# One-hot operands of an expert gate matrix: the first key's made by GpSimd instead of VectorE

## The chip, the cores and the metric

The kernel runs on one core of a Trainium2 chip, as one launch. The metric is the device time of one execution in microseconds, the median of several runs. TensorE, VectorE, ScalarE, GpSimd and SyncE each have an instruction queue of their own and run in its order; they meet at semaphores. In the profile they are PE (PEld is its weight load), DVE, ACT, POOL and SP.

## The reference, cut to what matters

A decoder layer for 1024 tokens (and 16 meta tokens) of width 1024 in float32: latent attention and retention side by side, merged, and then a mixer of 16384 single-neuron experts. The change lies in the mixer. Each token has 8 heads, and each head picks 16 experts by two keys, e1 and e2, from 0 to 127 each:

```python
q = (x @ w_peer_q).reshape(T, PEER_HEADS, PEER_DQ)
s1 = einsum('thd,kd->thk', q[..., :half], keys_1)      # 128 first keys
s2 = einsum('thd,kd->thk', q[..., half:], keys_2)      # 128 second keys
...
eidx = (e1 * 128 + e2).reshape(T, 8 * 16)              # 128 experts of one token
gates = softmax(sc).reshape(T, 8 * 16)
act = gelu(einsum('td,tkd->tk', x, peer_u[eidx]))
y = einsum('tk,tkd->td', gates * act, peer_v[eidx])
```

## The kernel before, in words

The 1024 tokens are 8 blocks of 128, in three groups: blocks 0 to 2, 3 and 4, 5 to 7. Attention, retention and merge run group after group. The experts are done in two ways.

*Blocks 0 to 2 gather.* For every token block and each of the 128 chosen experts, GpSimd issues an indirect DMA that fetches one row of peer_u or peer_v for each of the 128 tokens (`fetch` in `gathered`, L1065, tile `row`, 128 x 1024, four buffers, three fetched ahead). VectorE multiplies a row of peer_u with the tokens (L1082) or accumulates a row of peer_v into `acc` (L1087, `scalar_tensor_tensor` with `row` and `acc` as its two tiles). These VectorE instructions are pinned behind whatever was written to VectorE's queue just ahead of them (`keep_in_program_order`).

*Blocks 3 to 7 (640 tokens) are dense* (`dense`, L1128). For each first-key slice of 128 experts the scores of all 640 tokens are made by TensorE: the weights are split in a high part (`whi`, ScalarE, L218) and a low part (`wlo`, VectorE, L219), and three products (`mm3`, L246 to L248, tiles `tr`) are summed, in a 256-wide and a 384-wide piece; ScalarE applies the gelu (L1159). The scores of the first 48 slices are made ahead and stored to HBM (`gl_d`). Beside them the gate matrix is built: for each token a 128 x 128 matrix, first key by second key, with the gate where the token chose that expert. In the second half of `dense` the scores are multiplied with it (`gt`, read back from `gate_d`), and TensorE forms the output with peer_v (tiles `zacc`).

*The gate matrix* (`gate_matrix`, L1094) is a sum over the token's 128 choices, so it is a product: `oa` has for each choice (partition) a one at its first key, `ob` has the gate at its second key. Both compare a constant row of 0 to 127 (`iota`) with the key, a scalar for each partition (`kt`); `ob` multiplies with the gate (`gT`) as well. Of one token `oa` is the weight operand and `ob` the moving operand of TensorE's product (L1105, two instructions a token). Eight tokens make a step: two tiles `oa` and two `ob` of four tokens each, with four buffers each, so two steps fit. The products of a step are written after the operands of the next; ScalarE copies the result to `stage` (L1106), and every 32 tokens go to `gate_d` in one DMA from SyncE's queue.

*Order.* `pace` is called with a cost after each piece of foreground work and steps two background generators by credit: the routing and gate matrix of the dense blocks, and the gathers. A gate step yields 2.0, a gathered row 1.2. At the end of the 48 slices `finish(0)` drains what is left of the gate matrix. Within the dependencies the framework's scheduler then orders each engine's queue itself, by its own estimate of when an operand is ready; on TensorE the products of a token stand between score products.

Of the kernel before, what the change touches and what calls it, by code (L numbers as in the profile page):

```python
# [18 lines left out]
OP = mybir.AluOpType  # L19
# [124 lines left out]
def hybrid_layer(ctx: ExitStack, tc: tile.TileContext, out, a, dbg=None):  # L144
    nc = tc.nc
    V, S, T, G = nc.vector, nc.scalar, nc.tensor, nc.gpsimd
# [39 lines left out]
    def load_const(name, ap, shape):  # L186
        t = const.tile(shape, F32, name=name)
        nc.sync.dma_start(t, ap)
        return t
# [89 lines left out]
    def zacc(name="zacc"):  # L279
        return ps.tile([P, 2, 512], F32, name=name, tag="zacc", bufs=3)  # L280
# [813 lines left out]
    def gate_matrix(i, kt, gT, p):  # L1094

        stage = {}

        def products(t8, pairs):
            t0 = t8 // TS * TS
            if t8 == t0:  # L1100
                stage[0] = p.tile([P, P, TS], F32, name="stage", bufs=2)
            pg = zacc()
            for q, (oa, ob) in enumerate(pairs):
                for t in range(4):
                    T.matmul(pg[:, q, P * t:P * t + P], oa[:, t], ob[:, t], start=True, stop=True)  # L1105
            S.activation(stage[0][:, :, t8 - t0:t8 - t0 + 8].rearrange("p e (q t) -> p e q t", q=2),  # L1106
                         pg.rearrange("p q (t e) -> p e q t", t=4), AF.Copy)
            if t8 == t0 + TS - 8:
                nc.sync.dma_start(gate_d[(P * i + t0) // TS], stage[0].rearrange("p e t -> p (e t)"))

        pending = None
        for t8 in range(0, P, 8):
            pairs = []
            for q in range(2):
                oa = p.tile([P, 4, P], F32, name="oa", bufs=4)
                ob = p.tile([P, 4, P], F32, name="ob", bufs=4)
                for t in range(4):
                    k = t8 + 4 * q + t
                    V.tensor_scalar(oa[:, t], iota, kt[:, 0, k:k + 1], None, op0=OP.is_equal)  # L1119
                    V.tensor_scalar(ob[:, t], iota, kt[:, 1, k:k + 1], gT[:, k:k + 1], op0=OP.is_equal, op1=OP.mult)  # L1120
                pairs.append((oa, ob))
            if pending:
                products(*pending)
            pending = (t8, pairs)
            yield 2.0
        products(*pending)

    def dense(xT):  # L1128
# [33 lines left out]
        def routes():  # L1162

            kts, ktp = open_pool("ktl", "right")
            fcs, fc = open_pool("fcd", "right")
            n = len(last)
            top = top_tiles(n, fc)
            for h in range(H):
                first_top16(h, top, key_scores(queries(h, xT, n, fc), n))
                yield 1.85 * n  # L1170
            for i, b in enumerate(last):
                found = yield from choose(b, *top[i], fc, ktp)
                routed.append(found)
            fcs.close()
            pacing["rates"] = RATES[4]
            gms, gm = open_pool("gm")
            for i, (kt, gT) in enumerate(routed):
                yield from gate_matrix(i, kt, gT, gm)
            gms.close()
            kts.close()  # L1180
# [85 lines left out]
    iota = load_const("iota", a["c_iota"], [P, P])  # L1266
# [49 lines left out]
```

## Time and profile before

| | |
|---|---|
| median of 3 runs | 3613.85 us (3611.62 to 3617.17) |
| profiled execution | 3618.72 us, of which span 3616.9 us |
| busy: TensorE, VectorE, ScalarE, GpSimd | 3343.7, 2788.3, 1191.6, 1088.5 us |
| oa and ob (L1119, L1120) | 640 instructions each, from 1633.7 to 2037.1 us |

The span runs from the first instruction to the last. Busy time is the union of an engine's instructions, so instructions that overlap at their ends count once; a mean duration can then be longer than the distance from one start to the next. A TensorE instruction's end is modelled. The idle time of a group is that just before its instructions, with who released it.

### The profile page before, as it was taken

The numbers are of one execution on the slowest core, as the hardware profiler recorded it, in microseconds if no ns is written. First come the engines' busy times: TensorE is split into PE (matmuls) and PEld (weight loads), VectorE is DVE, ScalarE is ACT, GpSimd is POOL, SyncE is SP. The second block draws the span as 40 slices with busy tenths as digits, with TensorE's granted clock in tenths as the row PEclk, the third lists the DMA queues.
The fourth block names the chain that finished last, engine by engine and source line by source line (L and its number), as shares of the span: only waits on it lengthen the run. The fifth ranks groups of instructions, "written<-read, shape, count | busy, mean of one in ns | idle before, by whom it ended". The sixth has DMA issues, their size and how long they took to land.

```text
span 3616.9 us, 54537 instructions
## 1 busy us (share of the span) xinstructions
PE 3343.7 (92%) x20376; PEld 3023.5 (84%) x20376; DVE 2788.3 (77%) x6698; ACT 1191.6 (33%) x2017; POOL 1088.5 (30%) x772
## 2 busy tenths in 40 slices
PE   8999989998799998999898899999999989999999
PEld 7888988788677898998888687888788878887788
DVE  5645569997896666899999887787778777877776
ACT  3445334544355533233333222222222222222221
POOL 0000000112011121113333355454545544544454
PEclk9999999999899998999999999999999999999999
DMA  3322454467644376455666788898889888988886
GB/s 128 119 81 98 136 189 136 150 211 242 209 145 154 123 261 242 160 174 218 267 252 259 273 313 315 286 321 293 303 281 315 279 288 297 323 298 287 287 298 247
DMA packets 329257, 837.18 MB, mean 231 GB/s; under 512 B 45712, under 2 KB 140688, under 8 KB 326176
## 3 DMA queue, kind: packets, MB, share of 16 engines
q1 hardware_dynamic: 218400, 431.00, 35.4%
q0 software_dynamic: 110592, 402.70, 31.5%
q8 instruction: 160, 2.62, 0.3%
q14 instruction: 105, 0.86, 0.1%
HBM read 755.16 MB, written 78.43 MB: 230 GB/s over the span
## 4 chain that ended last, share of the span: by engine, by line
PE 42%; DVE 20%; issue 16%; DMA 11%; POOL 8%; ACT 3%; POOLq 0%; SPq 0%; DVEq 0%; ACTq 0%
PE zacc L246 9%; PE zacc L248 9%; PE zacc L247 9%; POOL row L1065 8%; DMA row<-in_peer_v_dram,eidx 7%; DVE ob L1120 4%; DVE oa L1119 3%; DVE wlo L219 3%; DVE acc L1087 3%; PE tr L246 3%; PE tr L247 2%; PE tr L248 2%; PE tr L765 2%; DMA gt<-gate_d 2%; PE sc L729 1%
## 5 line engine op out<-in xcount | busy, mean ns | idle before, releaser
L1065 POOL DMA_INDIRECT row<-in_peer_u_dram,eidx x384 | 494.6, 1288 | 1726.3 <-DVE row L1082 837.0
L218 ACT ACTIVATE whi<-raw 128x1024 fp32r<-128x1024 f32 (+2 forms) x508 | 520.7, 1026 | 1263.4 <-PE zacc L248 626.9
L219 DVE TENSOR_TENSOR wlo<-raw,whi 128x1024 fp32r<-128x1024 f32 (+2 forms) x508 | 599.3, 1180 | 328.4 <-ACT whi L218 327.3
L1065 POOL DMA_INDIRECT row<-in_peer_v_dram,eidx x384 | 593.7, 1546 | 772.9 <-DVE acc L1087 643.9
L246 PE MATMUL zacc<-whi,c_hi 128*128 128x512 f32 x1280 | 511.2, 399 | 75.3 <-ACT c_hi L218 59.2
L1087 DVE SCALAR_TENSOR_TENSOR acc<-row,dots,acc 128x1024 f32<-128x1024 f32 x384 | 481.7, 1279 | 92.9 <-DMA row<-in_peer_v_dram,eidx 92.2
L248 PE MATMUL zacc<-whi,c_lo 128*128 128x512 f32 x1280 | 509.1, 398 | 2.0 <-DVE c_lo L219 2.0
L247 PE MATMUL zacc<-wlo,c_hi 128*128 128x512 f32 x1280 | 507.9, 397 | 0.0
L1082 DVE SCALAR_TENSOR_TENSOR row<-row,xn 128x1024 f32<-128x1024 f32 x384 | 463.7, 1219 | 55.3 <-DMA row<-in_peer_u_dram,eidx 54.5
L246 PE MATMUL tr<-xT_hi,whi 128*128 128x384 f32 (+1 forms) x1216 | 417.0, 343 | 17.9 <-ACT gl L1159 16.8
L248 PE MATMUL tr<-xT_hi,wlo 128*128 128x384 f32 (+1 forms) x1216 | 413.9, 340 | 0.0
L247 PE MATMUL tr<-xT_lo,whi 128*128 128x384 f32 (+1 forms) x1216 | 411.8, 339 | 0.0
L246 PEld LDWEIGHTS zacc<-whi,c_hi 128*128 128x128 f32 x1280 | 246.9, 193 | 132.9 <-ACT c_hi L218 62.5
L248 PE MATMUL tr<-x_hi,wlo 128*128 128x256 f32 x1024 | 300.4, 293 | 37.3 <-DVE wlo L219 37.3
L246 PE MATMUL tr<-x_hi,whi 128*128 128x256 f32 x1024 | 299.5, 292 | 11.1 <-ACT whi L218 9.1
L247 PE MATMUL tr<-x_lo,whi 128*128 128x256 f32 x1024 | 297.0, 290 | 0.0
L248 PEld LDWEIGHTS zacc<-whi,c_lo 128*128 128x128 f32 x1280 | 245.7, 192 | 60.0 <-DVE c_lo L219 8.3
L247 PEld LDWEIGHTS zacc<-wlo,c_hi 128*128 128x128 f32 x1280 | 246.7, 193 | 51.3
L246 PE MATMUL zacc<-whi,hn_hi 128*128 128x256 f32 x832 | 251.5, 302 | 3.8 <-DVE vr L679 1.3
L246 PEld LDWEIGHTS tr<-xT_hi,whi 128*128 128x128 f32 x1216 | 232.4, 191 | 20.4 <-ACT gl L1159 18.0
L247 PE MATMUL zacc<-wlo,hn_hi 128*128 128x256 f32 x832 | 239.7, 288 | 1.4 <-DVE wlo L219 1.4
L248 PE MATMUL zacc<-whi,hn_lo 128*128 128x256 f32 x832 | 238.6, 287 | 0.0
(284 smaller groups left out, 6935.6 us busy)
## 6 DMA issues: line engine op xcount, KB each, us to landing
raw<-in_peer_ut_dram SPq DMA_DIRECT2D x128, 512.0 KB, 4.8
raw<-in_peer_vt_dram SPq DMA_DIRECT2D x128, 512.0 KB, 6.6
gate_d<-stage SPq DMA_DIRECT2D x20, 2048.0 KB, 7.4
gt<-gate_d SPq DMA_DIRECT2D x32, 1280.0 KB, 14.6
raw<-in_w_nat_dram SPq DMA_DIRECT2D x72, 512.0 KB, 3.5
raw<-in_w_z_dram SPq DMA_DIRECT2D x48, 512.0 KB, 3.3
gl_d<-gl SPq DMA_DIRECT2D x48, 320.0 KB, 2.2
gl<-gl_d SPq DMA_DIRECT2D x48, 320.0 KB, 6.3
```

The lines of the kernel that those rows point to most:

```text
L218: S.activation(hi, src, AF.Copy)
L219: V.tensor_tensor(lo, src, hi.bitcast(F32), OP.subtract)
L246: T.matmul(o, st[0], mv[0], start=first, stop=False)
L247: T.matmul(o, st[0], mv[1], start=False, stop=False)
L248: T.matmul(o, st[1], mv[0], start=False, stop=last)
L729: T.matmul(sc[:, c, 0:w], qh, kT[0:96, k0:k0 + w], start=True, stop=c < nch - 1)
L765: T.matmul(oo, vh[:, c + k], pT[:, k], start=False, stop=c + k == b)
L1065: G.indirect_dma_start(out=row, out_offset=None, in_=table, in_offset=bass.IndirectOffsetOnAxis(ap=eidx[:, k:k + 1], axis=0))
L1082: op = V.scalar_tensor_tensor(row, row, 1.0, xn, op0=OP.mult, op1=OP.mult, accum_out=dots[:, k:k + 1])
L1087: op = V.scalar_tensor_tensor(acc[k % 2], row, dots[:, k:k + 1], acc[k % 2], op0=OP.mult, op1=OP.add)
L1119: V.tensor_scalar(oa[:, t], iota, kt[:, 0, k:k + 1], None, op0=OP.is_equal)
L1120: V.tensor_scalar(ob[:, t], iota, kt[:, 1, k:k + 1], gT[:, k:k + 1], op0=OP.is_equal, op1=OP.mult)
```

## The change

One line. The `oa` tiles are filled by GpSimd instead of VectorE, with the same instruction, shape and operands; `ob` stays on VectorE, and nothing else is touched.

```diff
                 for t in range(4):
                     k = t8 + 4 * q + t
-                    V.tensor_scalar(oa[:, t], iota, kt[:, 0, k:k + 1], None, op0=OP.is_equal)
+                    G.tensor_scalar(oa[:, t], iota, kt[:, 0, k:k + 1], None, op0=OP.is_equal)
                     V.tensor_scalar(ob[:, t], iota, kt[:, 1, k:k + 1], gT[:, k:k + 1], op0=OP.is_equal, op1=OP.mult)
```

## Rows read from the trace of the kernel before

**Rows 1.** The page: busy time by engine, and GpSimd's row of the 40 slices.
```profile
PE 3343.7 (92%) x20376; PEld 3023.5 (84%) x20376; DVE 2788.3 (77%) x6698; ACT 1191.6 (33%) x2017; POOL 1088.5 (30%) x772
...
POOL 0000000112011121113333355454545544544454
```

**Rows 2.** Windows by stage: stretch, its length, busy time of each engine, clock, DMA.
```profile
core 0: us, PE busy (x) PEld busy (x) DVE busy (x) ACT busy (x) POOL busy (x), PEclk, DMA share, GB/s
1420.00:1633.00 213.00, 198.29 (x1250) 194.18 (x1249) 177.06 (x730) 67.86 (x101) 27.30 (x20) 0.96 0.50 169
1633.00:2040.00 407.00, 369.00 (x2606) 349.09 (x2605) 404.83 (x1378) 131.88 (x165) 130.72 (x70) 0.98 0.65 245
...
2170.00:3617.00 1447.00, 1360.11 (x7053) 1201.33 (x7051) 1106.66 (x1352) 334.68 (x454) 720.41 (x512) 0.97 0.85 295
```

**Rows 3.** Groups by line, 1633 to 2040 us: busy, mean ns | idle before, releasers.
```profile
L1120 DVE TENSOR_SCALAR ob<-iota,kt,gT 128x128 f32<-128x128 f32 x640 | 216.7, 339 | 0.0
L1105 PEld LDWEIGHTS zacc<-ob,oa 128*128 128x128 f32 x1280 | 186.9, 192 | 15.6 <-DVE ob L1120 8.3 <-issue 3.7 <-PE zacc L1105 0.4
L1119 DVE TENSOR_SCALAR oa<-iota,kt 128x128 f32<-128x128 f32 x640 | 182.2, 285 | 0.0
L1065 POOL DMA_INDIRECT row<-in_peer_v_dram,eidx x70 | 130.7, 1867 | 257.6 <-DVE acc L1087 245.4 <-DVE ob L1120 11.9 <-issue 0.3
L1087 DVE SCALAR_TENSOR_TENSOR acc<-row,dots,acc 128x1024 f32<-128x1024 f32 x72 | 88.5, 1274 | 2.2 <-DMA row<-in_peer_v_dram,eidx 2.2
...
L248 PE MATMUL tr<-x_hi,wlo 128*128 128x256 f32 x220 | 73.1, 332 | 35.5 <-DVE wlo L219 35.5
...
L219 DVE TENSOR_TENSOR wlo<-raw,whi 128x1024 fp32r<-128x1024 f32 x26 | 31.5, 1213 | 0.0
```

**Rows 4.** Chain of waits, 1633 to 2040 us, shares by line.
```profile
by line: DVE ob L1120 33.3%; DVE oa L1119 26.6%; DVE acc L1087 16.1%; issue 13.5%; DVE wlo L219 6.7%; DMA row<-in_peer_v_dram,eidx 3.4%; POOL row L1065 0.5%; DVEq L1087 0.0%; POOLq L1065 0.0%; DVEq L219 0.0%
```

**Rows 5.** Timeline of VectorE: start, length, then the instruction and its count.
```profile
1664.76 0.34 DVE L1120 TENSOR_SCALAR ob<-iota,kt,gT 128x128 f32<-128x128 f32 x1
1665.02 3.67 DVE L1087 SCALAR_TENSOR_TENSOR acc<-row,dots,acc 128x1024 f32<-128x1024 f32 x3
1668.61 1.22 DVE L219 TENSOR_TENSOR wlo<-raw,whi 128x1024 fp32r<-128x1024 f32 x1
1669.74 0.28 DVE L1119 TENSOR_SCALAR oa<-iota,kt 128x128 f32<-128x128 f32 x1
1669.94 0.34 DVE L1120 TENSOR_SCALAR ob<-iota,kt,gT 128x128 f32<-128x128 f32 x1
1670.19 0.28 DVE L1119 TENSOR_SCALAR oa<-iota,kt 128x128 f32<-128x128 f32 x1
```

**Rows 6.** Timeline of GpSimd in the same microseconds.
```profile
1666.57 4.07 POOL L1065 DMA_INDIRECT row<-in_peer_v_dram,eidx  x1 [10.08 <-DVE acc L1087]
1670.94 0.94 POOL L1065 DMA_INDIRECT row<-in_peer_v_dram,eidx  x1 [0.31 <-DVE ob L1120]
1672.19 0.94 POOL L1065 DMA_INDIRECT row<-in_peer_v_dram,eidx  x1 [0.30 <-DVE ob L1120]
```

**Rows 7.** Timeline of TensorE: products of the gates, then of the scores.
```profile
1704.86 1.95 PE L1105 MATMUL zacc<-ob,oa 128*128 128x128 f32 x16
...
2029.80 8.19 PE L1105 MATMUL zacc<-ob,oa 128*128 128x128 f32 x36
...
2039.45 0.28 PE L248 MATMUL tr<-x_hi,wlo 128*128 128x256 f32 x1
2039.57 0.28 PE L246 MATMUL tr<-x_hi,whi 128*128 128x256 f32 x1
...
2041.52 0.34 PE L246 MATMUL tr<-xT_hi,whi 128*128 128x384 f32 x1
2041.70 0.34 PE L247 MATMUL tr<-xT_lo,whi 128*128 128x384 f32 x1
```

**Rows 8.** Groups by line of GpSimd alone, whole span: its longest memset.
```profile
L1305 POOL MEMSET const-uint8-127<- 128x1 uint8 x1 | 0.1, 119 | 0.0
```

## The prediction, made before the changed kernel was run

> **What bounds the kernel now.** I read the page first, for the share of each engine and the slices: TensorE is busy 92% of the span, VectorE 77%, GpSimd 30%, and GpSimd does nothing but issue gathers [rows 1]. That is an average over stages, so the second view is the windows, cut at the first and last of the instructions that the diff touches [rows 2]. They lie between 1633 and 2040 us and nowhere else. In that stretch VectorE is busy 404.8 of 407 us, while TensorE has idle time of 38 us and GpSimd is busy 130.7. Before and after it VectorE has slack (177 of 213, 1107 of 1447). So VectorE bounds this one stretch, and the chain of waits agrees: of its time there 60% is oa and ob, 16% acc, 7% wlo [rows 4].
>
> The third view is the groups by line in the stretch [rows 3]: 640 oa, 640 ob, 72 accumulations of gathered rows (acc), 26 wlo (the low part of a score weight), 70 gathers. TensorE's named wait is for wlo, 35.5 us, because wlo queues behind the one-hot work. The fourth is the timeline, since mean durations overlap: an oa lasts 0.28 us but its ob starts 0.20 us after it, and the next oa 0.25 us after that ob [rows 5]. By starts, a token costs VectorE 0.196 + 0.256 = 0.452 us, an acc 1.20 (three in 3.59), a wlo 1.13. Sum: 640 x 0.452 = 289, 72 x 1.20 = 86, 26 x 1.13 = 29; together 404, which is the busy time found. TensorE's need by starts is less than its busy time says: 0.122 us for one product instruction (16 in 1.95), 0.118 for a 256-wide and 0.173 for a 384-wide score product [rows 7]. There are 1280 product instructions and, three products each, 660 score products of either width [rows 3]: 1280 x 0.122 + 660 x 0.118 + 660 x 0.173 = 156 + 78 + 114 = 348 us. In the last 28 us of the stretch TensorE counts as busy, but runs 36 products in 8.19 us, 0.228 each, at VectorE's pace [rows 7]. So a stretch in which VectorE is no limit could fall to 348, 59 us less.
>
> **The change, part by part.** *Removed:* 640 oa from VectorE, 640 x 0.196 = 125 us. What is left there is 640 x 0.256 + 86 + 29 = 279 us, so VectorE stops being the bound, and wlo comes in time.
>
> *Added:* 640 instructions on GpSimd, in one queue with the gathers. GpSimd's own load in the stretch has three terms. (a) 70 gathers: alone they follow each other in 1.25 us [rows 6], 70 x 1.25 = 88 us. (b) Time in which VectorE shuts GpSimd out. The first gather of a group lasts 4.07 us where its neighbours last 0.94: it starts at 1666.57, when the first acc of a run ends its work, and ends at 1670.64, some 0.9 us after the run of three acc and one wlo is over [rows 5, 6]. The neighbours lie fully beside oa and ob and are not lengthened. So acc and wlo, which read two SBUF tiles, hold GpSimd off for their whole length, 86 + 29 = 115 us; ob, which reads one, does not. I take it that an oa, which reads iota and kt, is held off in the same way as a gather. (c) A gather waits for the acc that frees its row; the oa behind it in the queue then wait too, and TensorE's weight load for these. Today this wait is 245.4 us in all [rows 3], but VectorE's queue is then full; with 128 us of slack acc comes early. Ends: 0 and 245; I take one ob (0.26 us) for each of some 30 groups, 8 us.
>
> The Trainium skill (SBUF — State Buffer, Who interferes with whom) says that a VectorE instruction with two SBUF inputs contends with a GpSimd one that reads SBUF, and that a tensor_scalar may run in a mode which takes both ports and then excludes GpSimd as well. The trace agrees with the first (4.07 against 0.94). By the second, ob would shut oa out too, and 164 us would be added to the sum below. The rows speak against it: wlo, with eight times the elements, is 0.93 us longer by starts than oa, 1.04 ns for each of the 896 more, and oa's 0.196 lies on that line with 0.06 us fixed; it doesn't run at twice the rate.
>
> *The disputed price, x, of one oa on GpSimd.* No row of before has GpSimd computing. Below: a memset of one element is 0.119 us [rows 8], and the same oa on VectorE 0.196 by starts. Above: the shortest gather, 0.94 us. The stretch takes 88 + 115 + 8 + 640x = 211 + 640x, if GpSimd bounds it; it equals today's 407 at x = 0.306, and TensorE's 348 at x = 0.214. Between ends this far apart I take the geometric middle of GpSimd's own two rows, sqrt(0.119 x 0.94) = 0.33 us; the row nearest to it is the same instruction with the same shape on VectorE, 1.7 times shorter. Then 211 + 640 x 0.33 = 422 us, 15 us more than today.
>
> The Trainium skill (GPSIMD Engine Reference, 3.1 Elementwise) has VectorE 1.96 times as fast in a two-input add; as an estimate from that page 0.196 x 1.96 = 0.38 us, the stretch 454, the change +47. The same page (4.1 Engine selection) calls one-input work roughly line-rate, which would put x near VectorE's 0.2 and give the fast rival. No run here shows either yet.
>
> *Moved or unchanged at nothing:* ob waits no longer behind oa; the products still need both, on separate instructions (weights from oa, moving data from ob), so TensorE gets no second wait on one instruction. Four oa tiles hold 16 tokens ahead, 16 x 0.54 = 8.7 us at TensorE's pace (348 us for 640 tokens), about as long as a run of three acc and a wlo with three gathers behind it (4.7 + 3.7 = 8.4 us): a stall there is inside GpSimd's sum already as long as GpSimd bounds, and costs up to some 10 us if TensorE does. SyncE's queue and the gate_d stores follow the stage and keep their number. After 2040 nothing changes: the gate matrix has to be whole there, so what the stretch gains or loses goes into the end one for one.
>
> **Sum.** The profiled execution took 3618.7 us for a span of 3616.9; +15 makes 3634. The median of the runs is 3613.85, 4.9 less, so 3629.
>
> **The rivals.** *GpSimd is quick (chance 0.37, faster).* x under 0.295. At 0.25 the stretch is 371, -36, 3578; at 0.2 TensorE bounds, -59, 3555. For it: GpSimd stood 245 us waiting in the stretch, and its memsets are short. Against: 115 us of lockout and 88 of gathers leave it only 204 of the 407. The point of decision is x = 0.306.
> *No change (0.13).* x from 0.295 to 0.317, or a quick GpSimd whose gain is eaten by oa waiting behind gathers: if a fifth of today's 245 us stays, it is 49 instead of 8, which turns x = 0.25 into 412. Within 7 us of before.
> *GpSimd is slow (0.12).* x of 0.44 and more: at 0.5 the stretch is 531, +124, 3738; at the upper end, 0.94, 813, +406, 4020. Here belongs the case that ob excludes oa (422 + 164 = 586, +179, 3793; 0.03 of the 0.12). For it: GpSimd's only sizable rows are near 1 us. Against: each of those fetches 128 rows of 4 KB from HBM, and an oa touches 128 elements a partition.
> *The forecast (0.38)* is x from 0.317 to 0.44: +7 to +86, 3621 to 3700.
>
> A measurement of this kernel can't tell less than about 0.2%, 7 us, from no change. So faster 0.37, same 0.13, slower 0.38 + 0.12 = 0.50. The forecast's own range is 3621 to 3700; the range for 8 in 10 reaches down to 3570 (x = 0.24), leaving out the quickest tenth, and up to 3700, leaving out the slow case.
>
> **What would show it.** In the changed profile the starts of neighbouring oa on GpSimd with no acc or wlo beside them give x at once; the formula then gives the length of the stretch from first to last ob. Step (b) is right if oa beside an acc are held for about its length, and wrong if they run on. Step (c) is the gathers' wait for acc: near 8 us or far above. VectorE should fall to some 280 us busy plus what it waits for oa's tiles; TensorE's wait should turn from wlo to oa. The forecast is wrong if x is under 0.3, if GpSimd computes beside acc, or if TensorE's idle time in the stretch falls under 30 us.

## The result, and the profile after

The changed kernel takes 3743.56 us in the median of four runs (3738.12 to 3759.37) against 3612.98 before: the ratio is 1.0367 (95% interval 1.0334 to 1.0399), 131 us slower. The direction was the forecast's; the size, 3629, and the range, up to 3700, were not.

The page of the changed kernel, busy time and GpSimd's slices [rows 1]:

```profile
PE 3414.8 (91%) x20376; PEld 3077.9 (82%) x20376; DVE 2690.9 (72%) x6058; ACT 1193.0 (32%) x2017; POOL 1452.6 (39%) x1412
...
POOL 0000001021011230169999955554445544455453
```

Its windows by stage, cut at the first oa and the last ob [rows 2]; columns as there:

```profile
1420.00:1625.00 205.00, 191.22 (x1201) 187.26 (x1201) 168.53 (x718) 66.02 (x98) 27.13 (x20) 0.95 0.49 167
1625.00:2172.00 547.00, 449.11 (x2641) 412.79 (x2640) 325.40 (x757) 133.95 (x167) 526.57 (x714) 0.83 0.51 189
2172.00:3742.00 1570.00, 1472.53 (x7682) 1300.99 (x7681) 1196.76 (x1440) 365.74 (x496) 761.08 (x556) 0.97 0.85 298
```

The groups by line in that stretch [rows 3]:

```profile
L1119 POOL TENSOR_SCALAR oa<-iota,kt 128x128 f32<-128x128 f32 x640 | 447.5, 714 | 1.2
...
L1105 PEld LDWEIGHTS zacc<-ob,oa 128*128 128x128 f32 x1280 | 197.0, 221 | 131.6 <-POOL oa L1119 108.8 <-issue 14.2
L1120 DVE TENSOR_SCALAR ob<-iota,kt,gT 128x128 f32<-128x128 f32 x640 | 191.1, 378 | 50.2 <-PE zacc L1105 50.2
L1087 DVE SCALAR_TENSOR_TENSOR acc<-row,dots,acc 128x1024 f32<-128x1024 f32 x76 | 98.2, 1319 | 55.2 <-DMA row<-in_peer_v_dram,eidx 55.2
L1065 POOL DMA_INDIRECT row<-in_peer_v_dram,eidx x74 | 81.4, 1100 | 28.7 <-DVE ob L1120 10.7 <-DVE acc L1087 9.5 <-issue 8.3
```

And the chain of waits in the stretch [rows 4]:

```profile
by line: POOL oa L1119 32.6%; PE zacc L1105 10.9%; DVE ob L1120 9.6%; PE tr L246 7.7%; PE tr L247 7.6%; PE tr L248 7.2%; DMA row<-in_peer_v_dram,eidx 5.8%; POOL row L1065 5.6%; issue 5.4%; DVE wlo L219 3.0%; ACT whi L218 2.1%; DVE acc L1087
```

The reader is to see that the bound has moved from VectorE to GpSimd. VectorE falls from 404.8 to 325.4 us busy in its stretch, GpSimd rises from 130.7 to 526.6 of 547 and waits only 20 us. The wait for wlo that TensorE had before is gone from the groups; its weight loads now wait 108.8 us for oa. The stretch from first oa to last ob is 546 us long against 404 before (+142); it starts 8 us earlier, with some 7 us of score products (counted with the prediction's prices) that stood ahead of it before and are now inside it. What follows the last ob, called the rest below, is 10 us shorter; its score products are the same in number, and no run shows why it is shorter. 142 - 8 - 10 = 124 us, the difference of the two spans.

The price of one oa on GpSimd is in the timeline. First a row of 16 with no acc or wlo beside them, and then 14 with two acc and a wlo beside them:

```profile
1654.35 9.31 POOL L1119 TENSOR_SCALAR oa<-iota,kt 128x128 f32<-128x128 f32 x16
...
1899.85 10.69 POOL L1119 TENSOR_SCALAR oa<-iota,kt 128x128 f32<-128x128 f32 x14
1910.71 1.09 POOL L1065 DMA_INDIRECT row<-in_peer_v_dram,eidx  x1 [0.17 <-DVE ob L1120]
1912.11 0.94 POOL L1065 DMA_INDIRECT row<-in_peer_v_dram,eidx  x1 [0.30 <-DVE ob L1120]
```

VectorE in the second of these places:

```profile
1900.21 2.58 DVE L1087 SCALAR_TENSOR_TENSOR acc<-row,dots,acc 128x1024 f32<-128x1024 f32 x2
1902.72 2.38 DVE L1120 TENSOR_SCALAR ob<-iota,kt,gT 128x128 f32<-128x128 f32 x8
1907.12 1.23 DVE L219 TENSOR_TENSOR wlo<-raw,whi 128x1024 fp32r<-128x1024 f32 x1 [2.02 <-ACT whi L218]
```

The 16 take 9.31 us, 0.58 each; over all pairs of neighbours the commonest distance from start to start is 0.578, alone and beside ob alike. The 14 would take 8.1 us at that rate and take 10.69: 2.6 more. Three of them are lengthened, from 0.59 to 1.52, 1.32 and 1.52 us, one for each acc and the wlo; the oa that was under way when the first acc began was not. So each of the three costs GpSimd 0.73 to 0.93 us, not its whole 1.2. Held off by acc and wlo, an oa lasts 0.714 in the mean instead of 0.592, 640 x 0.122 = 78 us in all. So GpSimd's stretch adds up: 640 x 0.578 = 370, held off 78, gathers 79 (526.6 - 447.5; some 11 of these are gathers held off too), idle 20; together 547.

### The profile page after: what moved, and what is told of

It reads as the page before. It is cut to its first block, busy times and chain, and to the rows that moved or that the text cites. A ratio compares the mean times of both kernels' runs of the same rounds, so it can differ in the third digit from the quotient of the medians.

```text
span 3741.3 us, 55114 instructions
## 1 busy us (share of the span) xinstructions
PE 3414.8 (91%) x20376; PEld 3077.9 (82%) x20376; DVE 2690.9 (72%) x6058; ACT 1193.0 (32%) x2017; POOL 1452.6 (39%) x1412
## 4 chain that ended last, share of the span: by engine, by line
PE 54%; DVE 14%; DMA 11%; issue 9%; POOL 9%; ACT 3%; POOLq 0%; SPq 0%; DVEq 0%; ACTq 0%
PE zacc L246 10%; PE zacc L248 10%; PE zacc L247 10%; DMA row<-in_peer_v_dram,eidx 5%; PE tr L246 5%; PE tr L247 5%; POOL oa L1119 5%; PE tr L248 5%; POOL row L1065 4%; DVE wlo L219 3%; DMA gt<-gate_d 3%; PE tr L765 2%; PE zacc L1105 2%; DVE ob L1120 1%; PE sc L729 1%
## 5 line engine op out<-in xcount | busy, mean ns | idle before, releaser
L1065 POOL DMA_INDIRECT row<-in_peer_v_dram,eidx x384 | 513.7, 1338 | 531.6 <-DVE acc L1087 408.2
L1119 POOL TENSOR_SCALAR oa<-iota,kt 128x128 f32<-128x128 f32 x640 | 447.5, 714 | 1.2
L1105 PE MATMUL zacc<-ob,oa 128*128 128x128 f32 x1280 | 235.5, 336 | 95.6 <-POOL oa L1119 86.4
L1105 PEld LDWEIGHTS zacc<-ob,oa 128*128 128x128 f32 x1280 | 197.0, 221 | 131.6 <-POOL oa L1119 108.8
```

The lines of the kernel that those rows point to most:

```text
L1065: G.indirect_dma_start(out=row, out_offset=None, in_=table, in_offset=bass.IndirectOffsetOnAxis(ap=eidx[:, k:k + 1], axis=0))
L1119: G.tensor_scalar(oa[:, t], iota, kt[:, 0, k:k + 1], None, op0=OP.is_equal)
```

## The experiments

The theory: GpSimd's queue bounds the stretch of the gate matrix, by the sum just given. Rival 1: it is the mix, oa behind gathers in one queue and the new order of TensorE's queue, and not the amount. Rival 2: TensorE itself, whose granted clock falls from 0.98 to 0.83 in the stretch. "Stretch" is from the first to the last oa or ob in the profiled run; times are medians, each beside runs of the kernel before on the same chip.

**Half of the oa back on VectorE (e1_half), or three quarters (e2_quarter).**

```diff
-                    G.tensor_scalar(oa[:, t], iota, kt[:, 0, k:k + 1], None, op0=OP.is_equal)
+                    (G if t % 2 else V).tensor_scalar(oa[:, t], iota, kt[:, 0, k:k + 1], None, op0=OP.is_equal)
```

(For a quarter: `G if t == 3 else V`.)

> Every second oa is made by GpSimd, the others by VectorE. Theory (GpSimd's queue bounds the stretch of the gate matrix: 0.58 us an oa, 1.25 a gather, about 75 us held off by acc and wlo): GpSimd 320 x 0.58 + 88 + 75 = 349 us, VectorE 405 - 320 x 0.196 = 342, TensorE 348, so the stretch is 350 to 380 us against 407 before and 547 after, and the time 3560 to 3590, faster than before. Rival 1 (not the amount but the mix: oa behind gathers in one queue, and the new order of TensorE's queue, make TensorE wait): about half of the loss stays, stretch about 470, time about 3675. Rival 2 (TensorE's lower granted clock is the cost): between the two, with a granted clock near 0.9 in the stretch.

> One oa in four is made by GpSimd. Theory: GpSimd 160 x 0.58 + 88 + 75 = 256 us, VectorE 405 - 160 x 0.196 = 374, which bounds: stretch 374 to 385, time 3580 to 3592, a little slower than with half. Rival 1: a quarter of the loss, stretch about 440, time about 3645.

Half: 3597.25 us against 3616.41, ratio 0.9943 (0.9924 to 0.9963). A quarter: 3604.87, 0.9973 (0.9960 to 0.9987). Both are faster than before by less than 1%, where rival 1 had them 30 to 60 us slower, so that rival falls: the mix of oa and gathers in one queue does not by itself bring the loss. But the times miss the theory's (3560 to 3590 and 3580 to 3592), and the stretch did not shrink as it said: 402 and 398 us against 404, not 350 to 385. In the half kernel it holds 12 us more of score products, and GpSimd's price is higher than in the sum. A row of GpSimd's timeline in e1_half:

```profile
1797.22 8.86 POOL L1119 TENSOR_SCALAR oa<-iota,kt 128x128 f32<-128x128 f32 x10
```

And its group in the stretch:

```profile
L1119 POOL TENSOR_SCALAR oa<-iota,kt 128x128 f32<-128x128 f32 x320 | 293.6, 930 | 4.8 <-PE zacc L1105 3.0
```

These ten take 0.89 us each, with two acc among them. Where VectorE makes oa and ob in turn beside it, an oa on GpSimd lasts 0.72 in the median and not 0.59; with acc and wlo the mean is 0.93, and GpSimd is busy 375 of 402 us. The sum of 349 that I expected was 26 us short by this. The other 27 us GpSimd is idle; TensorE (373 us busy) and VectorE (369) are nearly as full, and no run shows a single bound of this stretch. In the quarter kernel VectorE bounds as expected, busy 393 of 398 us, but 19 more than the 374 worked out: its own 480 oa are busy 149 us beside GpSimd's, where three quarters of the 182 of before [rows 3] would be 137.

**Four tokens in one instruction on VectorE (e3_tt_vector).** Nothing on GpSimd.

```diff
+                k0 = t8 + 4 * q
+                V.tensor_tensor(oa, iota.unsqueeze(1).to_broadcast([P, 4, P]),
+                                kt[:, 0, k0:k0 + 4].unsqueeze(2).to_broadcast([P, 4, P]), OP.is_equal)
                 for t in range(4):
                     k = t8 + 4 * q + t
-                    G.tensor_scalar(oa[:, t], iota, kt[:, 0, k:k + 1], None, op0=OP.is_equal)
```

> All oa on VectorE, but four tokens in one tensor_tensor of 128x512 with broadcast operands instead of four tensor_scalar. By the slope of wlo against oa it takes 0.06 + 512 x 0.00104 = 0.59 us for four tokens against 4 x 0.196 = 0.78, 160 x 0.19 = 31 us less on VectorE. If VectorE's time bounds the stretch before (theory): stretch about 376, time about 3582. If the stretch before was set by order and waits: no change, 3613.

Measured: 3596.57 us, ratio 0.9955 (0.9932 to 0.9978), stretch 380 us; the new instruction is 0.60 us from start to start. The stretch came out near the expected 376; the time fell by some 16 to 20 us of the 31, and not to 3582. This bears out the reading of before: there VectorE bounds, and of the time taken from it more than half comes back.

**What 0.58 us are made of (e4_two64).** Each oa in two instructions of 64 columns.

```diff
-                    G.tensor_scalar(oa[:, t], iota, kt[:, 0, k:k + 1], None, op0=OP.is_equal)
+                    for c in (slice(0, 64), slice(64, 128)):
+                        G.tensor_scalar(oa[:, t, c], iota[:, c], kt[:, 0, k:k + 1], None, op0=OP.is_equal)
```

> All oa on GpSimd, each in two instructions of 64 columns. What the 0.58 us are made of: if the price is per instruction, starts stay 0.58 apart, 640 x 0.58 = 370 us more, stretch about 915 and time about 4110; if it is per element, starts are 0.29 apart and stretch and time stay (547, 3744); half and half gives 0.43, stretch about 730, time about 3930. In each case the theory has the time move by 640 times the second instruction's price; the rivals (order, clock) have it move less.

Measured: 3939.42 us in one run, stretch 738. The case "half and half" (730, 3930) is what came. The first 47 of a row of its GpSimd timeline, with only ob beside them:

```profile
2320.79 19.45 POOL L1120 TENSOR_SCALAR oa<-iota,kt 128x64 f32<-128x64 f32 x47
```

And the group in the stretch:

```profile
L1120 POOL TENSOR_SCALAR oa<-iota,kt 128x64 f32<-128x64 f32 x1280 | 645.8, 539 | 1.1
```

47 in 19.45 us is 0.41 each; the commonest distance with nothing on VectorE beside is 0.412. So 64 columns more cost 0.578 - 0.412 = 0.166 us, 2.6 ns a column, and what remains, 0.246 us, is fixed, if the cost is a straight line between these two sizes. The oa need 1280 x 0.412 = 527 us instead of 370, +157; they are busy 645.8 us, so acc, wlo and in part ob hold them back by 118 us instead of 78, +41. Together +198; gathers and idle time are 6 us less, and the stretch grew by 192. The rivals had it move by less than the price, and fall.

**Less work for TensorE (e5_onethird).** Two of the three score products are left out in the first 48 slices.

```diff
-                    mm3(pu[:, :w], (hi[:, c], lo[:, c]), [t[:, j] for t in x], j == 0, j == KD - 1)
+                    if gate_time[0]:
+                        T.matmul(pu[:, :w], lo[:, c], x[0][:, j], start=j == 0, stop=j == KD - 1)
+                    else:
+                        mm3(pu[:, :w], (hi[:, c], lo[:, c]), [t[:, j] for t in x], j == 0, j == KD - 1)
...
         finish(0)
+        gate_time[0] = False
```

> The changed kernel, with two of the three score products left out in the first 48 slices (only the low-part product with the high part of x stays), so TensorE has some 130 us less to do in the stretch of the gate matrix. Theory (GpSimd's queue bounds): the stretch stays, 530 to 550 us against 546. Rival (TensorE is what is slow, by its granted clock of 0.83 in the stretch and by its new order): the stretch falls by 100 us or more, under 450.

The window of the stretch in e5_onethird:

```profile
1616.00:2168.00 552.00, 395.73 (x1705) 330.69 (x1703) 323.90 (x753) 128.44 (x162) 528.39 (x711) 0.72 0.51 183
```

TensorE runs 1705 products instead of 2641, at a granted clock of 0.72, the lowest of the stretches shown, and the stretch is 552 us, 547 with all products (time 3741.25, one run). Rival 2 falls: with a third of the score work and a still lower clock the stretch is the same, so neither TensorE's work nor its clock sets it.

**No gathers beside the gate matrix (e6_nogather), and the same with oa on VectorE (e7_nogather_vector).**

```diff
-RATES = ((0.0, 0.0), (0.5, 0.2), (0.3, 0.3), (0.8, 0.2), (0.8, 0.45), (0.0, 0.5))
+RATES = ((0.0, 0.0), (0.5, 0.2), (0.3, 0.3), (0.8, 0.2), (0.8, 0.0), (0.0, 0.58))
```

> The changed kernel, with no gathers stepped while the gate matrix is built (that stage's second rate 0 instead of 0.45; they come later, at a rate of 0.58 instead of 0.5). GpSimd then has only oa in the stretch, and VectorE no acc. Theory with the three terms (640 x 0.578 = 370, gathers 91, held off 75 to 85): the stretch is 370 + 15 for wlo = 380 to 395 us. Theory with x alone, where the other terms are no sum but hidden: 540. Rival (order and waits of TensorE): above 450. The time has no clean forecast, as the gathers must go elsewhere; about 3600 if they find room.

> The kernel before (oa on VectorE), with the same two rates. VectorE has 289 + 29 = 318 us in the stretch, so TensorE bounds at 348: stretch 350 to 365 us, 40 less than before. If the gathers find room later, the time is 3570 to 3585; if the stage behind has no room, the gain is given back there and the time is about 3613.

Windows, stretch and rest, of e6_nogather:

```profile
1627.00:2045.00 418.00, 395.90 (x2651) 368.38 (x2649) 243.58 (x692) 133.91 (x167) 415.81 (x649) 0.95 0.44 169
2045.00:3745.00 1700.00, 1504.49 (x7681) 1321.91 (x7680) 1275.36 (x1505) 362.81 (x496) 875.00 (x620) 0.95 0.84 294
```

And of e7_nogather_vector:

```profile
1636.00:1988.00 352.00, 351.95 (x2639) 345.97 (x2637) 325.23 (x1311) 133.50 (x167) 4.91 (x4) 1.00 0.48 185
1988.00:3707.00 1719.00, 1503.87 (x7630) 1322.43 (x7629) 1285.46 (x1514) 361.27 (x493) 887.19 (x624) 0.94 0.84 293
```

With oa on GpSimd the stretch falls from 547 to 418 us: the gathers and the acc were a true part of the sum, and rival 1, which had it above 450, falls here too. It stays over the 380 to 395 expected, because wlo and the 11 acc that remained held GpSimd off for 38 us and not 15, and 8 gathers that remained took 8; GpSimd is busy 415.8 of 418. With oa on VectorE the stretch is 352 us with TensorE busy all of it, the 348 that the prediction had worked out for TensorE. But both lose in time: 3746.66 us (one run), and 3704.30, ratio 1.0240 (1.0209 to 1.0270). The rest then holds 64 and 66 gathers more and is 131 and 140 us longer, 2.0 and 2.1 us for each; that the edit also sets the rest's own rate to 0.58 was not tried alone. "Given back later" was the right half of that expectation, and more than given back.

**The best split (e8_mix).** One oa tile in four on GpSimd, the others as in e3_tt_vector.

```diff
+                on_g = q == 1 and t8 % 16 == 8
+                if not on_g:
+                    k0 = t8 + 4 * q
+                    V.tensor_tensor(oa, iota.unsqueeze(1).to_broadcast([P, 4, P]),
+                                    kt[:, 0, k0:k0 + 4].unsqueeze(2).to_broadcast([P, 4, P]), OP.is_equal)
...
+                    if on_g:
+                        G.tensor_scalar(oa[:, t], iota, kt[:, 0, k:k + 1], None, op0=OP.is_equal)
```

> One oa tile in four is made by GpSimd with tensor_scalar (160 of 640 oa), the others by VectorE with one tensor_tensor for four tokens (0.60 us, as measured in e3_tt_vector). VectorE 120 x 0.60 + 640 x 0.256 + 115 = 351 us, GpSimd 160 x 0.58 to 0.71 + 91 + 75 = 259 to 280, TensorE 348: stretch 355 to 370, time 3575 to 3590, faster than each half alone (3597). If what is left is TensorE's own time, no better than 3590.

Measured: 3593.37 us, ratio 0.9931 (0.9908 to 0.9955), stretch 386 us. It beats both kernels; against e1_half (0.9943) and e3_tt_vector (0.9955) the intervals overlap. The stretch is 16 us over the expected range, with VectorE busy 364 and not 351 us and idle for the other 22, nearly all of it waiting for products to free an oa tile. The 128x512 instruction takes 0.60 us from start to start as in e3; ob is what is longer beside GpSimd's oa, 0.31 us from one to the next in the median instead of 0.256.

**More gathers in the stretch (e9_before_rate70, e10_mix_rate70, e11_mix_rate90).** e6 and e7 had suggested that the rest is bound by the gathers left to it; the edit is 0.70 or 0.90 for the 0.45 in `RATES`, in the kernel before and in e8_mix.

> The kernel before with the gathers' rate in the gate stage at 0.70 instead of 0.45. Theory from e6 and e7 (the stage behind is bound by the gathers left to it, 2.1 us for each one more; a gather in the stretch costs VectorE one acc, 1.2 us): some 40 gathers more in the stretch, stretch 404 + 48 = 452, the rest 1579 - 84 = 1495, time about 3577. Rival (the stage behind is bound by TensorE, and only more gathers than now hurt it): stretch +48, rest as before, time about 3660.

> The kernel of e8_mix with that rate at 0.70. VectorE 365 + 48 = 413 us, GpSimd 262 + 40 x 1.4 and what acc holds it off, about 345: stretch 410 to 425, rest 1575 - 84 = 1490, time about 3545. Rival: stretch +30, rest as before, time about 3625.

> The kernel of e8_mix with that rate at 0.90, some 72 gathers more in the stretch. VectorE 365 + 86 = 451 us, GpSimd about 390: stretch 450 to 470, rest 1575 - 150 = 1425, time about 3515. If the rest reaches TensorE's own time on the way, it falls by less and the time is 3530 to 3560. Rival: time about 3665.

Measured: 3659.06 (1.0126, 1.0100 to 1.0151), 3648.86 (1.0100, 1.0072 to 1.0129) and 3771.85 (1.0439, 1.0401 to 1.0478), all slower. In e9 the stretch grew to 451 us, as worked out (452), but the rest is 1570 with 38 gathers less, against 1579 before, and not 1495. In e10 it is 1568 with 520 gathers left and in e11 1580 with 490. My theory of the rest falls, and its rival's "rest as before" holds in all three: with fewer than the 558 gathers of before it stays at 1568 to 1580 us, in a stage where TensorE is busy 94% of the time (1360 of 1447 us in the longest part of it [rows 2]). That TensorE sets it was not tested. The stretch missed too where GpSimd has oa as well: 444 us in e10 (410 to 425 expected) and 550 in e11 (450 to 470), so that e11 is 107 us over its rival's time. In e11's stretch VectorE is busy only 445 us:

```profile
L1087 DVE SCALAR_TENSOR_TENSOR acc<-row,dots,acc 128x1024 f32<-128x1024 f32 x120 | 149.3, 1286 | 92.2 <-DMA row<-in_peer_v_dram,eidx 92.2
```

Its acc waits 92 us for rows, which my sums had at nothing (in e10 it is 31). Of the rates tried, 0, 0.45, 0.70 and 0.90, 0.45 is the best.

## Why the prediction was wrong

*What bounds before* was right. VectorE bounds the stretch (e3: shorten its instructions, and the stretch follows), TensorE's own need is 348 us (e7: 352, busy throughout), and acc costs what was said (e9: 38 gathers more, 451 us for 452).

*Removed:* right in kind. VectorE stops being the bound and the wait for wlo goes. The 279 us left on it came as 325: ob is busy 191 us and not 164, and acc and wlo 134 and not 115.

*The price x* is the step that failed: 0.33 us, "the geometric middle of GpSimd's own two rows". It is 0.578, so 640 of them are 370 us and not 211, +159. The two rows, a memset of one column and a gather, say nothing of how long a column takes; a middle of two unrelated things was no estimate. The case in which it fell, x of 0.44 and more, had a chance of 0.12, and its example, x = 0.5, gave 3738 us, close to the 3743.56 measured by luck: its x is 50 us too small in all, its time held off 37 too large, and it did not have the 18 us that the earlier start and the shorter rest give back. The Trainium skill's ratio (GPSIMD Engine Reference, 3.1 Elementwise), 1.96 for a two-input add, is too kind here: 0.578 to 0.196 is 2.9. Its word that one-input work is roughly line-rate (4.1 Engine selection) does not hold in this run: 2.6 ns a column on GpSimd (e4), where a whole oa on VectorE comes to 1.5 ns a column (0.196 us for 128).

*Held off (b):* acc and wlo hold oa off, as the row of 14 shows, but not for their whole length; the size was 115 us where 78 came. An oa already under way is not stopped, so each acc or wlo costs 0.73 to 0.93 us there; and 32 of the 50 unbroken runs of acc in the stretch are now a single one (2 of 29 before), since acc waits for its rows (55.2 us), so that this happens at nearly each. With the 11 us of the gathers it is 89 us for 76 acc and 29 wlo, 0.85 us each.

*Gathers (a) and waits (c):* 88 + 8 = 96 us expected, 79 + 20 = 99 found. Right.

Together 159 - 37 + 3 = +125 us, from the 422 of the sum to 547.

*One for one:* the stretch's 142 us came to 124 in the span, as its start moved 8 us ahead and the rest became 10 shorter. The prediction had both at nothing; why the rest is shorter stays open.

*The other rivals.* That GpSimd is quick is refuted. That ob shuts oa out is refuted too: an oa beside ob alone starts 0.578 after the last, as one beside nothing. The prediction's reason against it was weaker than this: a line through wlo and oa has only two points, and any two lie on a line.

## What to carry to other kernels

Work moved to an idle engine is paid at that engine's price, and an average of 30% busy hides what its queue already holds in the one stage where the work lies, here 157 us of gathers and of time held off: sum the new engine's stage before the old one's saving. When no row has the operation on the new engine, the honest range is as wide as its nearest rows, and moving a quarter first puts the price into a trace (0.72 us an oa in e2_quarter). Here half of the move gains 0.6%, and the whole loses 3.7%.

## What the runs showed of the hardware

GpSimd takes 0.246 us for a tensor_scalar of this kind plus 2.6 ns a column, by the two sizes that ran (128 and 64 columns). Contention also went the other way than I had looked for. In the changed kernel VectorE's ob, which reads one SBUF tile, is 0.256 us from the next in the median beside a gather (131 pairs), and 0.306 beside GpSimd's oa (392 pairs). An oa on GpSimd lasts 0.59 us beside ob alone, and 0.72 beside VectorE's oa and ob in turn (220 in e1_half). The Trainium skill (SBUF — State Buffer, Who interferes with whom) says that a VectorE instruction with one SBUF input outside its two-port modes does not contend; in these runs both sides are slowed, and they don't show which of the two conditions is not met, or whether the rule itself fails. That acc and wlo contend with a GpSimd instruction, as it says of two SBUF inputs, is borne out by e6_nogather and the changed kernel; what each cost GpSimd there was 0.85 to 0.95 us in the mean, of the 1.1 to 1.2 that it takes.
